# Hybrid decoder step on one Trainium2 core: elementwise work moved from GpSimd to VectorE and ScalarE

## The chip, the cores and the metric

The kernel runs on one core of one Trainium2 chip. The core has five engines that run side by side and wait for each other through semaphores: TensorE (PE in the profile; its weight loads are PEld), VectorE (DVE), ScalarE (ACT), GpSimd (POOL) and SyncE (SP), whose queue issues the kernel's DMAs. The metric is the time of one execution on the device in microseconds (us), smaller is better.

## What is computed

One layer of a decoder over a prompt of 2048 tokens (width 1024) and one decode step for 8 samples. Cut to what matters here:

```
h = rmsnorm(x, g_norm1) * (1 + sc1) + sh1
qkv, z, beta_in, a_in, aq, ak, av, iq, ik, iw = split(h @ w_in)
conv = silu(sum(w_conv[i] * xcat[:, i:i + t] for i in range(4)))   # xcat: three carried rows, then qkv
gq, gk, gv = split(conv); gq = l2norm(gq) * 128 ** -0.5; gk = l2norm(gk)
o_gdn, s_new = delta_rule(gq, gk, gv, g, beta, s0)                 # chunked, with a triangular solve
o_gdn = rmsnorm(o_gdn, g_gdn_norm) * silu(z)
aq, ak, iq, ik = partial_rope(...)
o_att = sparse_attn(aq, ak, av, iq, ik, iw)                        # scores, the best 256 keys, softmax
x = x + ga1 * (concat(o_gdn, o_att) @ w_out)
h2 = rmsnorm(x, g_norm2) * (1 + sc2) + sh2
gate, up = split(h2 @ w_ffn_in)
x = x + ga2 * ((silu(gate) * up) @ w_ffn_out)
```

Everything is float32. The large matrix products are made of two parts of each operand: a high part (the value as TensorE's float32r takes it) and a low part (the value minus its high part). Three products, high by high, high by low and low by high, are added up.

## The kernel before

**Tiling and staging.** The prompt is worked in four groups of 512 tokens. Phase 1 makes the modulation vectors, and for each group `project` (normalise, transpose, the input projection, the short convolution, rope) and `chunks` (the delta rule, in four chunks of 128 tokens, two of them interleaved). For the middle groups two blocks of attention (`first_attn`) and the later modulation vectors (`modulate`) stand between them. Phase 2 runs, for each group, the attention of the next four blocks of 128 tokens and then `ffn` (output projection, norm, SwiGLU, residual); the decode samples' attention and state step (`sample_steps`) stands ahead of the last `ffn`.

**Order.** All tiles come from pools with a fixed number of buffers per tag. The program is written in the order above, but a planner (`TileContext(schedule_with_timeline_sim=True)`) lays out each engine's instructions in an order that it finds by simulating the engines; then every engine works through its own list. An operation that changes its engine can therefore change the order of its neighbours.

**The weight path.** `weights` (L130 to L146) fetches a tile of 128 x 512 weights: SP loads it into `wr` (two buffers), ScalarE makes the high part with a cast (L141), GpSimd subtracts it for the low part (L142), both into `wi` (three buffers). The 56 tiles of the input projection are written back to DRAM in split form (`kept`) and only loaded for the later groups. The matmuls are those of `mm3` (L157 to L159), and of `mm_s` (L173, L174) for the few rows of the samples and the modulation. The buffer `wr` is free for the next load when the low part has been made.

**The steps around the change.** `norm_T` (L344) scales each row (L353), and for each of eight tiles transposes (L357), applies the modulation on VectorE into `ca` (two buffers, L359), casts on ScalarE (L360) and subtracts for the low part (L361). `conv` (L615) keeps three columns per channel block in `hist`; it puts them in front of the new columns in `raw` (L619, L620), saves the last three (L621), and does the four taps on VectorE (L624, L626). `rope` (L601) is four small operations on the rotated columns (L610 to L613). `tok` takes a block of projected tokens: for z it multiplies by the norm's gain (L645), and for the indexer queries it makes high and low parts of 256 columns (L689, L690) that TensorE then transposes (L694). `narrow` (L514) makes the gates in a chain of very small VectorE operations up to L553, which TensorE waits for at L559, and ropes the indexer keys.

`chunk` and `state` are the delta rule. A chunk transposes q, k and v (L729), squares them (L745), takes sums and a power (L747, L190), scales (L752, L754, L757), makes decay masks (L774, L776), builds a triangular matrix (L787, L788, L792, L793) and inverts it in six levels of matmuls (L800, L805, L806); `state` then updates the state (L849, L850) and normalises the output (L855 to L860).

**What stays.** The power of `rpow` (L190) stays on GpSimd, as do the low parts of the attention output (L1362) and of the gated hidden tile (L1425), and the residual adds of the FFN (L1353), each behind a VectorE multiplication (L1352).

Of the kernel before, what the change touches and what calls it, by code (L numbers as in the profile page):

```python
# [24 lines left out]
F32 = mybir.dt.float32  # L25
# [4 lines left out]
OP = mybir.AluOpType  # L30
# [10 lines left out]
H = 4  # L41
# [66 lines left out]
class K:  # L108
# [21 lines left out]
    def weights(self, src, key=None):  # L130

        nc = self.nc
        w = self.wp.tile([128, 2, 512], F32R, name="wi", tag="wi", bufs=WI)
        if key in self.kept:
            nc.sync.dma_start(w.bitcast(F32), self.kept[key])
            return w[:, 0], w[:, 1]
        wr = self.wp.tile([128, 512], F32, name="wr", tag="wr", bufs=WR)
        n = 512 // len(src)
        for j, s in enumerate(src):
            nc.sync.dma_start(wr[:, j * n:(j + 1) * n], s)  # L140
        nc.scalar.copy(w[:, 0], wr)  # L141
        nc.gpsimd.tensor_tensor(w[:, 1], wr, w[:, 0].bitcast(F32), op=OP.subtract)  # L142
        if key is not None:
            self.kept[key] = self.dr.tile([128, 2, 512], F32, name="kept")
            nc.sync.dma_start(self.kept[key], w.bitcast(F32))
        return w[:, 0], w[:, 1]  # L146
# [197 lines left out]
    def norm_T(self, pool, xt, nblk, Amul, Badd, hh, hl, tag, ptag, pbufs):  # L344

        nc = self.nc
        ss = pool.tile([128, nblk], F32, name=tag + "ss", tag=tag + "ss")
        for t in range(nblk):
            self.squares(pool, ss[:, t:t + 1], xt[:, t, :])
        r = self.rpow(pool, ss, nblk, 1.0 / D, EPS, tag)  # L350
        xn = xt
        for t in range(nblk):
            nc.vector.tensor_scalar(xn[:, t, :], xt[:, t, :], r[:, t:t + 1], None, op0=OP.mult)  # L353
        for k in range(KB):
            pt = self.ps.tile([128, 512], F32, name=ptag, tag=ptag, bufs=pbufs)
            for t in range(nblk):
                nc.tensor.transpose(pt[:, t * 128:(t + 1) * 128], xn[:, t, k * 128:(k + 1) * 128], self.id)  # L357
            h = self.p.tile([128, 512], F32, name="ca", tag="ca", bufs=2)
            nc.vector.tensor_scalar(h, pt, Amul[:, k, 0:1], Badd[:, k, 0:1], op0=OP.mult, op1=OP.add)  # L359
            nc.scalar.copy(hh[:, k, :], h)  # L360
            nc.gpsimd.tensor_tensor(hl[:, k, :], h, hh[:, k, :].bitcast(F32), op=OP.subtract)  # L361

    def norm_T_s(self, pool, xs, Amul, Badd, tag, ptag, pbufs):
        nc = self.nc
# [236 lines left out]
    def rope(self, x, tab, blk, rows, nh, half, tag):  # L601

        nc, p = self.nc, self.p1
        t = p.tile([128, 2, 8, 2, 8] if half == 8 else [128, 2, 4, 2, 16], F32, name="rope", tag="rope", bufs=1)
        xv = x[:, :, 0:2 * half].rearrange("p h (a c) -> p h a c", a=2)
        cosv = tab[:rows, blk, 0, :]
        b4 = lambda a: a.unsqueeze(1).unsqueeze(1).to_broadcast([rows, nh, 2, half])
        b3 = lambda a: a.unsqueeze(1).to_broadcast([rows, nh, half])
        pc, pn = t[:rows, 0, :nh], t[:rows, 1, :nh]
        nc.gpsimd.tensor_tensor(pc, xv, b4(cosv), op=OP.mult)  # L610
        nc.gpsimd.tensor_tensor(pn[:, :, 0, :], xv[:, :, 1, :], b3(tab[:rows, blk, 1, :]), op=OP.mult)
        nc.gpsimd.tensor_tensor(pn[:, :, 1, :], xv[:, :, 0, :], b3(tab[:rows, blk, 2, :]), op=OP.mult)
        nc.gpsimd.tensor_tensor(xv, pc, pn, op=OP.add)  # L613

    def conv(self, g, m, pd):  # L615

        nc, p = self.nc, self.p1
        raw = self.m("raw")
        nc.gpsimd.tensor_copy(raw[:, 0:3], self.hist[:, m, :])  # L619
        nc.scalar.copy(raw[:, 3:515], pd)  # L620
        nc.gpsimd.tensor_copy(self.hist[:, m, :], raw[:, 512:515])  # L621
        w = lambda i: self.cv[:, 64 + i * 12 + m:65 + i * 12 + m]
        a = self.p.tile([128, 512], F32, name="ca", tag="ca", bufs=2)
        nc.vector.tensor_scalar(a, raw[:, 0:512], w(0), None, op0=OP.mult)  # L624
        for i in range(1, 4):
            nc.vector.scalar_tensor_tensor(a, raw[:, i:i + 512], w(i), a, op0=OP.mult, op1=OP.add)  # L626
        th = self.th("cth")
        nc.scalar.activation(th, a, AF.Tanh, scale=0.5)
        nc.vector.scalar_tensor_tensor(th, th, 1.0, a, op0=OP.add, op1=OP.mult)
        nc.sync.dma_start(self.cT_d[g * 4:g * 4 + 4, :, m, :].rearrange("c p n -> p c n"), th.rearrange("p (c n) -> p c n", c=4))  # L630

    def tok(self, what, blk, pd, rows):
        nc, p, O = self.nc, self.p1, self.O
# [3 lines left out]
        if what == "z":  # L637
            th = self.th("cth")
            nc.scalar.activation(th[R], pd[R], AF.Tanh, scale=0.5)
            nc.vector.scalar_tensor_tensor(th[R], th[R], 1.0, pd[R], op0=OP.add, op1=OP.mult)  # L640
            if samp:
                nc.sync.dma_start(self.gzs_d, th[R])
            else:
                v = th.rearrange("p (h e) -> p h e", h=H)
                nc.gpsimd.tensor_tensor(v, v, self.gg.unsqueeze(1).to_broadcast([128, H, 128]), op=OP.mult)  # L645
                nc.sync.dma_start(self.gz_d[blk], th)
            return
        a = self.m("tk")[:, :512]
# [29 lines left out]
        else:  # L678
# [7 lines left out]
            for b in range(2):  # L686
                x = self.m("iqs", F32R)[:, :512].rearrange("p (h a c) -> p h a c", h=4, a=2)
                v = a[:, b * 256:(b + 1) * 256].rearrange("p (h c) -> p h c", h=4)
                nc.scalar.copy(x[:, :, 0, :], v)  # L689
                nc.gpsimd.tensor_tensor(x[:, :, 1, :], v, x[:, :, 0, :].bitcast(F32), op=OP.subtract)  # L690
                if b:
                    pt = self.ps.tile([128, 512], F32, name="d", tag="d", bufs=4)
                for h in range(4):
                    nc.tensor.transpose(pt[:, h * 128:(h + 1) * 128], x[:, h].bitcast(F32).rearrange("p a c -> p (a c)"), self.id)  # L694
                q = self.m("qo")[:, :512]
                nc.scalar.copy(q, pt)
                nc.sync.dma_start(self.iqT_d[blk, :, b * 512:(b + 1) * 512], q)
# [10 lines left out]
    def chunk(self, g, c, keep):  # L708

        nc, p = self.nc, self.p1  # L710
        n = g * 4 + c
        c4 = slice(c * 4, c * 4 + 4)
# [9 lines left out]
        v4 = lambda a: a.rearrange("p (h e) -> p h e", h=H)  # L722
        col = lambda a: a.unsqueeze(2).to_broadcast([128, a.shape[1], 128])
# [11 lines left out]
        qk = t("qk", 1024)  # L735
        v = t("v")
# [5 lines left out]
        yield  # L742
        kq = p.tile([128, H, 2, 128], F32, name="kq", bufs=2)
        sq = kq.rearrange("p h a e -> p (h a e)")
        nc.gpsimd.tensor_tensor(sq, qk, qk, op=OP.mult)  # L745
        ss = p.tile([128, 8], F32, name="ss8", bufs=2)
        nc.vector.tensor_reduce(ss, sq.rearrange("p (h e) -> p h e", h=8), op=OP.add, axis=AX.X)  # L747

        rn = self.rpow(p, ss, 8, 1.0, 4 * EPS, "rn")
        nc.vector.tensor_scalar(rn[:, 0:4], rn[:, 0:4], 128.0 ** -0.5, None, op0=OP.mult)  # L750
        qk8 = qk.rearrange("p (h e) -> p h e", h=8)
        nc.gpsimd.tensor_tensor(qk8, qk8, col(rn), op=OP.mult)  # L752
        qe = t("qe")
        nc.gpsimd.tensor_tensor(v4(qe), qk8[:, 0:4], col(self.gc[:, 3, c4]), op=OP.mult)  # L754
        yield
        kd = t("kd")
        nc.gpsimd.tensor_tensor(v4(kd), qk8[:, 4:8], col(self.gc[:, 4, c4]), op=OP.mult)  # L757
        transposed(lambda h: qk8[:, 4 + h, :], kq[:, :, 0, :], "s")
        yield
        transposed(lambda h: qk8[:, h, :], kq[:, :, 1, :], "v")  # L760
# [10 lines left out]
            nc.vector.tensor_scalar(dec[:, hs(h)], pg[:, hs(h)], self.gc[:, 2, c * 4 + h:c * 4 + h + 1], 0.0,  # L771
                                    op0=OP.add, op1=OP.min)
        nc.scalar.activation(dec, dec, AF.Exp)
        nc.gpsimd.tensor_tensor(v4(dec), v4(dec), self.u.unsqueeze(1).to_broadcast([128, H, 128]), op=OP.mult)  # L774
        decb = t("decb")
        nc.gpsimd.tensor_tensor(v4(decb), v4(dec), col(self.nbeta[:, c4]), op=OP.mult)  # L776
        yield
        NT, AT = t("NT"), t("AT")
        for a in range(2):
# [9 lines left out]
            yield  # L789

        E, Dm = t("E"), t("Dm")
        nc.gpsimd.tensor_tensor(v4(E), v4(NT), self.l1.unsqueeze(1).to_broadcast([128, H, 128]), op=OP.mult)  # L792
        nc.gpsimd.tensor_tensor(v4(E), v4(E), self.id.unsqueeze(1).to_broadcast([128, H, 128]), op=OP.add)  # L793
        transposed(lambda h: E[:, hs(h)], v4(Dm), "s")
        yield
        Y = t("Y")
# [15 lines left out]
    def state(self, g, c, kq, v, E, AT, qeT, kd):  # L812
# [33 lines left out]
        pu = P()  # L846
        for h in range(H):
            nc.tensor.matmul(pu[:, hs(h)], kd[:, hs(h)], vn[:, hs(h)], start=True, stop=True)
        nc.gpsimd.tensor_tensor(S2, S, col(self.gc[:, 5, c4]), op=OP.mult)  # L849
        nc.vector.tensor_tensor(S2, S2, v4(pu), op=OP.add)  # L850

        o = t("qe")
        nc.scalar.copy(o, po)
        sq2 = R
        nc.gpsimd.tensor_tensor(sq2, o, o, op=OP.mult)  # L855
        s4 = p.tile([128, 4], F32, name="ss4", bufs=2)
        nc.vector.tensor_reduce(s4, v4(sq2), op=OP.add, axis=AX.X)
        r4 = self.rpow(p, s4, 4, 1.0 / 128, EPS, "r4")
        nc.gpsimd.tensor_tensor(v4(o), v4(o), col(r4), op=OP.mult)
        nc.gpsimd.tensor_tensor(o, o, gz, op=OP.mult)  # L860
        oT = t("dec")
        pt = P()
        for h in range(H):
# [630 lines left out]
```

## Time and profile before

| | us |
|---|---|
| median of three runs | 4083.31 (4079.41 to 4086.87) |
| the profiled execution, whole | 4080.21 |
| its span, from the first to the last instruction | 4078.1 |

The profile is of one execution. Busy times are per engine; a share is of the span. In a group's row stand the source line, the engine, the operation, output <- inputs with their shapes, the count, the busy time in us and the mean in ns, and after the second bar the idle time of the engine just before these instructions, with what ended it. A wait's row reads: who waited <- for whom: us in total, times, longest. A stretch's row gives its two ends, its length, and the busy time of each engine in it with the number of instructions, then the granted TensorE clock (1.00 is full speed), the share of the DMA engines and their GB/s.

### The profile page before, as it was taken

The numbers are of one execution on the slowest core, as the hardware profiler recorded it, in microseconds if no ns is written. First come the engines' busy times: TensorE is split into PE (matmuls) and PEld (weight loads), VectorE is DVE, ScalarE is ACT, GpSimd is POOL, SyncE is SP. The second block draws the span as 40 slices with busy tenths as digits, with TensorE's granted clock in tenths as the row PEclk, the third lists the DMA queues.
The fourth block names the chain that finished last, engine by engine and source line by source line (L and its number), as shares of the span: only waits on it lengthen the run. The fifth ranks groups of instructions, "written<-read, shape, count | busy, mean of one in ns | idle before, by whom it ended". The sixth has DMA issues, their size and how long they took to land. (4 is left out here: it accounts for less than half of the span.)

```text
span 4078.1 us, 51174 instructions
## 1 busy us (share of the span) xinstructions
PE 3699.3 (91%) x17420; PEld 2852.2 (70%) x17420; DVE 1873.0 (46%) x3492; ACT 1357.3 (33%) x2583; POOL 1992.0 (49%) x1897
## 2 busy tenths in 40 slices
PE   8888988899798879999998999998999996889997
PEld 4766877777686657677776777876877754467775
DVE  2423432441355223866668757387671238022123
ACT  2233223322332333333344443344433331132222
POOL 3366234432621575544564555564555552246555
PEclk9899999999899889999999999999999996989998
DMA  6653453373346334355535333234333333332222
GB/s 233 209 204 118 128 199 113 118 239 132 124 157 215 103 94 139 101 145 163 154 105 172 92 95 102 88 119 162 93 103 101 91 101 126 133 100 81 80 78 71
DMA packets 368313, 528.21 MB, mean 130 GB/s; under 512 B 45612, under 2 KB 246353, under 8 KB 365986
## 3 DMA queue, kind: packets, MB, share of 16 engines
q1 hardware_dynamic: 368042, 524.86, 40.5%
q8 instruction: 139, 2.28, 0.2%
q14 instruction: 132, 1.08, 0.1%
HBM read 427.33 MB, written 116.36 MB: 133 GB/s over the span
## 5 line engine op out<-in xcount | busy, mean ns | idle before, releaser
L142 POOL TENSOR_TENSOR wi<-wr,wi 128x512 fp32r<-128x512 f32 x712 | 937.6, 1323 | 1060.3 <-ACT wi L141 1030.7
L141 ACT CAST wi<-wr 128x512 fp32r<-128x512 f32 x712 | 439.5, 620 | 1118.7 <-PE d L159 345.6
L157 PE MATMUL d<-hh,wi 128*128 128x512 f32 x1792 | 736.0, 411 | 23.4 <-DVE tm L1352 7.0
L158 PE MATMUL d<-hl,wi 128*128 128x512 f32 x1792 | 717.2, 400 | 0.0
L159 PE MATMUL d<-hh,wi 128*128 128x512 f32 x1792 | 653.4, 403 | 0.0
L157 PEld LDWEIGHTS d<-hh,wi 128*128 128x128 f32 x1792 | 339.6, 190 | 118.9 <-DVE tm L1352 11.3
L159 PEld LDWEIGHTS d<-hh,wi 128*128 128x128 f32 x1792 | 338.3, 189 | 89.1 <-issue 6.7
L158 PEld LDWEIGHTS d<-hl,wi 128*128 128x128 f32 x1792 | 339.5, 189 | 77.5 <-issue 5.5
L1353 POOL TENSOR_TENSOR xt<-xt,tm 128x512 f32<-128x512 f32 x224 | 302.4, 1366 | 50.5 <-DVE tm L1352 34.3
L157 PE MATMUL d<-wi,hh 128*128 128x512 f32 x768 | 297.2, 411 | 24.5 <-DMA wi<-kept 15.5
L1245 DVE SCALAR_TENSOR_TENSOR sc<-rl,iw,sc 128x512 f32<-128x512 f32 (+3 forms) x224 | 222.2, 992 | 196.3 <-ACT rl L1238 187.4
L158 PE MATMUL d<-wi,hh 128*128 128x512 f32 x768 | 308.9, 402 | 0.2 <-POOL wi L142 0.2
L159 PE MATMUL d<-wi,hl 128*128 128x512 f32 x768 | 306.0, 400 | 0.0
L158 PE MATMUL d<-wi,ah 128*128 128x512 f32 x704 | 275.9, 395 | 0.9 <-POOL wi L142 0.9
L159 PE MATMUL d<-wi,al 128*128 128x512 f32 x704 | 271.4, 397 | 0.0
L157 PE MATMUL d<-wi,ah 128*128 128x512 f32 x704 | 256.5, 407 | 7.6 <-ACT ah L1424 3.6
L1352 DVE TENSOR_TENSOR tm<-d,row 128x512 f32<-128x512 f32 x224 | 150.1, 685 | 221.9 <-PE d L159 160.4
L1419 DVE SCALAR_TENSOR_TENSOR th<-th,d 128x512 f32<-128x512 f32 x88 | 58.1, 682 | 373.5 <-ACT th L1418 373.3
L806 DVE COPY_PREDICATED Dm<-cl,g 128x512 f32<-128x512 uint8 x96 | 70.0, 731 | 312.0 <-PE g L805 311.8
L1238 ACT ACTIVATE rl<-s 128x512 f32<-128x512 f32 (+3 forms) x288 | 148.1, 543 | 149.2 <-PE s L1236 110.4
L1139 DVE TENSOR_SCALAR_CACHE_REDUCE bias<-sc,sv 128x640 bf16<-128x640 f32 (+11 forms) x120 | 193.3, 1611 | 3.2
L157 PEld LDWEIGHTS d<-wi,hh 128*128 128x128 f32 x768 | 146.5, 192 | 66.4 <-DMA wi<-kept 17.8
(504 smaller groups left out, 6398.7 us busy)
## 6 DMA issues: line engine op xcount, KB each, us to landing
wr<-in_w_ffn_in_dram SPq DMA_DIRECT2D x704, 128.0 KB, 2.3
wi<-kept SPq DMA_DIRECT2D x168, 512.0 KB, 4.1
wr<-in_w_ffn_out_dram SPq DMA_DIRECT2D x176, 256.0 KB, 2.7
kept<-wi SPq DMA_DIRECT2D x56, 512.0 KB, 2.9
xt<-in_x_prompt_dram SPq DMA_DIRECT2D x8, 2048.0 KB, 7.6
wr<-in_w_ada_dram SPq DMA_DIRECT2D x64, 256.0 KB, 2.8
wr<-in_w_out_dram SPq DMA_DIRECT2D x64, 256.0 KB, 2.6
wr<-in_w_in_dram SPq DMA_DIRECT2D x56, 256.0 KB, 3.7
```

The source lines that it names most:

```text
L141: nc.scalar.copy(w[:, 0], wr)
L142: nc.gpsimd.tensor_tensor(w[:, 1], wr, w[:, 0].bitcast(F32), op=OP.subtract)
L157: nc.tensor.matmul(out, wh, xh, start=start, stop=False, **kw)
L158: nc.tensor.matmul(out, wh, xl, start=False, stop=False, **kw)
L159: nc.tensor.matmul(out, wl, xh, start=False, stop=stop, **kw)
L806: nc.vector.copy_predicated(v4(Dm), self.cl[:, lv, :].unsqueeze(1).to_broadcast([128, H, 128]), v4(pp))
L1139: nc.vector.tensor_scalar(c, s, t, None, op0=OP.is_ge, op1=OP.add, accum_out=cnt)
L1238: nc.scalar.activation(r[:, :w], ps[:, :w], AF.Relu)
L1245: nc.vector.scalar_tensor_tensor(s, r[:, :w], iw, s, op0=OP.mult, op1=OP.add)
L1352: nc.vector.tensor_tensor(tm[:rows], pd[:rows], rw, op=OP.mult)
L1353: nc.gpsimd.tensor_tensor(xt, xt, tm[:rows], op=OP.add)
L1419: nc.vector.scalar_tensor_tensor(th, th, 1.0, pd[j], op0=OP.add, op1=OP.mult)
```

## The change

Twenty lines of GpSimd work go to VectorE: the low part of the weights (L142) and of the normalised tile (L361), the four operations of rope (L610 to L613), the gain of z (L645), the low part of the indexer queries (L690), and in the delta rule L745, L752, L754, L757, L774, L776, L792, L793, L849, L855, L859 and L860. The two copies of the convolution's carry (L619, L621) go to ScalarE, and the second one reads the matmul's result in PSUM rather than the copied tile. Operands and shapes of the moved operations stay the same.

```diff
-        nc.gpsimd.tensor_tensor(w[:, 1], wr, w[:, 0].bitcast(F32), op=OP.subtract)
+        nc.vector.tensor_tensor(w[:, 1], wr, w[:, 0].bitcast(F32), op=OP.subtract)
...
-            nc.gpsimd.tensor_tensor(hl[:, k, :], h, hh[:, k, :].bitcast(F32), op=OP.subtract)
+            nc.vector.tensor_tensor(hl[:, k, :], h, hh[:, k, :].bitcast(F32), op=OP.subtract)
...
-        nc.gpsimd.tensor_tensor(pc, xv, b4(cosv), op=OP.mult)
+        nc.vector.tensor_tensor(pc, xv, b4(cosv), op=OP.mult)
...
-        nc.gpsimd.tensor_copy(raw[:, 0:3], self.hist[:, m, :])
+        nc.scalar.copy(raw[:, 0:3], self.hist[:, m, :])
         nc.scalar.copy(raw[:, 3:515], pd)
-        nc.gpsimd.tensor_copy(self.hist[:, m, :], raw[:, 512:515])
+        nc.scalar.copy(self.hist[:, m, :], pd[:, 509:512])
...
-                nc.gpsimd.tensor_tensor(v, v, self.gg.unsqueeze(1).to_broadcast([128, H, 128]), op=OP.mult)
+                nc.vector.tensor_tensor(v, v, self.gg.unsqueeze(1).to_broadcast([128, H, 128]), op=OP.mult)
...
-                nc.gpsimd.tensor_tensor(x[:, :, 1, :], v, x[:, :, 0, :].bitcast(F32), op=OP.subtract)
+                nc.vector.tensor_tensor(x[:, :, 1, :], v, x[:, :, 0, :].bitcast(F32), op=OP.subtract)
...
-        nc.gpsimd.tensor_tensor(sq, qk, qk, op=OP.mult)
+        nc.vector.tensor_tensor(sq, qk, qk, op=OP.mult)
...
-        nc.gpsimd.tensor_tensor(v4(E), v4(NT), self.l1.unsqueeze(1).to_broadcast([128, H, 128]), op=OP.mult)
-        nc.gpsimd.tensor_tensor(v4(E), v4(E), self.id.unsqueeze(1).to_broadcast([128, H, 128]), op=OP.add)
+        nc.vector.tensor_tensor(v4(E), v4(NT), self.l1.unsqueeze(1).to_broadcast([128, H, 128]), op=OP.mult)
+        nc.vector.tensor_tensor(v4(E), v4(E), self.id.unsqueeze(1).to_broadcast([128, H, 128]), op=OP.add)
...
-        nc.gpsimd.tensor_tensor(S2, S, col(self.gc[:, 5, c4]), op=OP.mult)
+        nc.vector.tensor_tensor(S2, S, col(self.gc[:, 5, c4]), op=OP.mult)
```

The lines of rope and of the delta rule that aren't printed here change in the same way.

More of the change, by code (lines that the diff above doesn't have):

```diff
@@ L609, in rope @@
         pc, pn = t[:rows, 0, :nh], t[:rows, 1, :nh]
-        nc.gpsimd.tensor_tensor(pc, xv, b4(cosv), op=OP.mult)
-        nc.gpsimd.tensor_tensor(pn[:, :, 0, :], xv[:, :, 1, :], b3(tab[:rows, blk, 1, :]), op=OP.mult)
-        nc.gpsimd.tensor_tensor(pn[:, :, 1, :], xv[:, :, 0, :], b3(tab[:rows, blk, 2, :]), op=OP.mult)
-        nc.gpsimd.tensor_tensor(xv, pc, pn, op=OP.add)
+        nc.vector.tensor_tensor(pc, xv, b4(cosv), op=OP.mult)
+        nc.vector.tensor_tensor(pn[:, :, 0, :], xv[:, :, 1, :], b3(tab[:rows, blk, 1, :]), op=OP.mult)
+        nc.vector.tensor_tensor(pn[:, :, 1, :], xv[:, :, 0, :], b3(tab[:rows, blk, 2, :]), op=OP.mult)
+        nc.vector.tensor_tensor(xv, pc, pn, op=OP.add)
     def conv(self, g, m, pd):
@@ L751, in chunk @@
         qk8 = qk.rearrange("p (h e) -> p h e", h=8)
-        nc.gpsimd.tensor_tensor(qk8, qk8, col(rn), op=OP.mult)
+        nc.vector.tensor_tensor(qk8, qk8, col(rn), op=OP.mult)
         qe = t("qe")
-        nc.gpsimd.tensor_tensor(v4(qe), qk8[:, 0:4], col(self.gc[:, 3, c4]), op=OP.mult)
+        nc.vector.tensor_tensor(v4(qe), qk8[:, 0:4], col(self.gc[:, 3, c4]), op=OP.mult)
         yield
         kd = t("kd")
-        nc.gpsimd.tensor_tensor(v4(kd), qk8[:, 4:8], col(self.gc[:, 4, c4]), op=OP.mult)
+        nc.vector.tensor_tensor(v4(kd), qk8[:, 4:8], col(self.gc[:, 4, c4]), op=OP.mult)
         transposed(lambda h: qk8[:, 4 + h, :], kq[:, :, 0, :], "s")
@@ L773, in chunk @@
         nc.scalar.activation(dec, dec, AF.Exp)
-        nc.gpsimd.tensor_tensor(v4(dec), v4(dec), self.u.unsqueeze(1).to_broadcast([128, H, 128]), op=OP.mult)
+        nc.vector.tensor_tensor(v4(dec), v4(dec), self.u.unsqueeze(1).to_broadcast([128, H, 128]), op=OP.mult)
         decb = t("decb")
-        nc.gpsimd.tensor_tensor(v4(decb), v4(dec), col(self.nbeta[:, c4]), op=OP.mult)
+        nc.vector.tensor_tensor(v4(decb), v4(dec), col(self.nbeta[:, c4]), op=OP.mult)
         yield
@@ L854, in state @@
         sq2 = R
-        nc.gpsimd.tensor_tensor(sq2, o, o, op=OP.mult)
+        nc.vector.tensor_tensor(sq2, o, o, op=OP.mult)
         s4 = p.tile([128, 4], F32, name="ss4", bufs=2)
@@ L858, in state @@
         r4 = self.rpow(p, s4, 4, 1.0 / 128, EPS, "r4")
-        nc.gpsimd.tensor_tensor(v4(o), v4(o), col(r4), op=OP.mult)
-        nc.gpsimd.tensor_tensor(o, o, gz, op=OP.mult)
+        nc.vector.tensor_tensor(v4(o), v4(o), col(r4), op=OP.mult)
+        nc.vector.tensor_tensor(o, o, gz, op=OP.mult)
         oT = t("dec")
```

## The prediction

> **What bounds the kernel now.** I read the page's busy lines first, then the busy table over chosen stretches, then PE's waits, then the groups by form for prices.
>
> ```profile
> span 4078.1 us, 51174 instructions
> PE 3699.3 (91%) x17420; PEld 2852.2 (70%) x17420; DVE 1873.0 (46%) x3492; ACT 1357.3 (33%) x2583; POOL 1992.0 (49%) x1897
> ```
>
> PE is busy for 91% of the span, so at most 4078.1 - 3699.3 = 379 us could be won by feeding it better. VectorE (DVE) and GpSimd (POOL) are each busy about half of the time, but not in the same stretches (columns: the stretch and its length, then PE, PEld, DVE, ACT and POOL busy, granted clock, DMA share, GB/s):
>
> ```profile
> 0.00:1600.00 1600.00, 1390.53 (x7454) 1118.25 (x7455) 574.91 (x1255) 489.96 (x987) 697.70 (x863) 0.93 0.47 157
> 350.00:400.00 50.00, 31.72 (x205) 26.67 (x205) 24.82 (x45) 18.21 (x36) 43.35 (x47) 0.83 0.18 56
> 700.00:750.00 50.00, 39.02 (x201) 29.19 (x201) 18.37 (x37) 18.67 (x32) 44.63 (x38) 0.83 0.47 144
> 1050.00:1100.00 50.00, 36.72 (x195) 27.87 (x196) 17.00 (x36) 18.85 (x32) 44.29 (x38) 0.86 0.51 156
> 1440.00:1490.00 50.00, 34.24 (x154) 23.40 (x154) 12.91 (x34) 16.98 (x30) 45.17 (x38) 0.77 0.36 106
> 1600.00:3300.00 1700.00, 1631.81 (x7099) 1260.72 (x7098) 1049.26 (x1844) 663.16 (x1207) 907.10 (x706) 0.99 0.39 118
> 2100.00:2300.00 200.00, 181.91 (x797) 136.70 (x796) 165.30 (x299) 94.51 (x183) 106.90 (x78) 0.98 0.42 138
> 2800.00:2900.00 100.00, 93.14 (x400) 69.71 (x399) 85.23 (x149) 45.89 (x85) 39.37 (x31) 0.95 0.40 129
> 2900.00:3000.00 100.00, 100.00 (x430) 78.30 (x430) 69.92 (x107) 38.85 (x67) 56.79 (x43) 1.00 0.31 92
> ```
>
> Of the 379 us, 209 lie in the first 1600 us (projections, delta rule, modulation) and 68 in the next 1700 (attention beside the FFN). Four **seams** of 50 us in the first stage, between one group's projection and the next, have POOL 87 to 90% busy and PE at 63 to 78%, with the granted clock down to 0.77: there POOL is the bound. From 1600 on PE is the bound, and DVE comes nearest to a second one: 83% in 2100-2300 and 85% in 2800-2900.
>
> **The change part by part.** First the prices: each row has its count, then busy us and mean ns.
>
> ```profile
> L142 POOL TENSOR_TENSOR wi<-wr,wi 128x512 fp32r<-128x512 f32 x712 | 937.6, 1323 | 1060.3 <-ACT wi L141 1030.7 <-DMA wr<-in_w_ffn_in_dram 7.8 <-DMA kept<-wi 5.8
> L752 POOL TENSOR_TENSOR qk<-qk,rnz 128x1024 f32<-128x1024 f32 x16 | 30.3, 1896 | 0.3
> ```
>
> ```profile
> L850 DVE TENSOR_TENSOR S<-S,s 128x512 f32<-128x512 f32 x16 | 11.0, 685 | 43.5 <-PE s L848 43.5
> L747 DVE TENSOR_REDUCE ss<-kq 128x8 f32<-128x1024 f32 x16 | 19.4, 1215 | 4.9 <-POOL kq L745 4.9
> L787 DVE TENSOR_TENSOR NT<-g,decb 128x256 f32<-128x256 f32 x32 | 13.5, 422 | 43.2 <-POOL decb L776 23.4 <-PE g L782 19.9
> L592 DVE TENSOR_TENSOR iks<-ik,iks 128x128 fp32r<-128x128 f32 x16 | 5.3, 330 | 1.1 <-ACT iks L591 1.1
> L549 DVE TENSOR_TENSOR spw<-spw 128x16 f32<-128x16 f32 x21 | 3.6, 171 | 0.5
> ```
>
> A moved 128x512 operation goes from 1.32 us on POOL (L142) to about 0.685 on DVE (L850; it reads one input from PSUM, and L592 and L549 with both inputs in SBUF lie on the same slope), a 128x1024 one from 1.90 to about 1.215, 256 columns to 0.42. DVE gains 712 (L142) + 64 (L361) + 160 (ten lines of the delta rule x16) + 16 (L645) = 952 x 0.685 = 652 us, 32 x 1.215 = 39 (L745, L752), 32 x 0.42 = 13 (L690), and for the 64 ropes of four small operations, between 0.17 and 0.33 each, about 62: 766 us in all. That makes 1873 + 766 = 2639, 65% of the span; over the whole run DVE isn't full. What counts is each stage.
>
> *Seams and waits for POOL.* PE's longest waits in the first 1600 us (total us, times, longest):
>
> ```profile
> PE d L694 <- POOL iqs L690: 27.0, 6, 6.8
> PE d L174 <- POOL wi L142: 19.6, 15, 2.9
> ...
> PE g L729 <- POOL qk L752: 16.4, 9, 5.1
> PE d L559 <- DVE gt L553: 13.9, 1, 13.9
> PE d L173 <- ACT wi L141: 10.9, 15, 1.8
> ...
> PE g L729 <- POOL E L793: 9.1, 5, 4.8
> ```
>
> The POOL waits and the L173 wait behind them are 83.0 us. If these are serial chains, they shrink as their operations do, to about 0.55 (0.685/1.323 and 1.215/1.896, mixed): 46% of 83 = 38 us gone, and the low clock that goes with the gaps gives a little more; 46 as an outer end. If they are load, the seams' work only changes engines: DVE gets 0.55 x POOL on top of its own, 24.8 + 23.8 = 48.6 of 50 where POOL had 43.4, then 42.9 for 44.6, 41.4 for 44.3 and 37.8 for 45.2; in sum 170.7 for 177.4, a gain of 7 us, and the first seam even loses 5. A wait in front of a single L694 is a chain, but DVE's queue now carries the two chunks, the ropes and the weights in one order, and each wait for ScalarE that POOL used to sit out holds them all. I take a point between the ends, **-25** (ends -46 and +5).
>
> *The narrow chain.* L559's 13.9 us are DVE working through a chain of tiny operations. The key ropes add 5 x 4 operations of 0.171 us to the same queue: **+3** (0 to +3.4). For groups 1 to 3 other matmuls hide it.
>
> *norm_T.* DVE makes the scaled tile (0.81 us) and now the low part too: 1.49 us per tile. Today POOL sets that pace, as two of its low parts start 3598.94 and 3601.79, 2.85 us apart:
>
> ```profile
> 3598.94 2.49 POOL L361 TENSOR_TENSOR hl<-ca,hh 128x512 fp32r<-128x512 f32 x2 [0.35 <-ACT hh L360]
> ...
> 3601.47 0.81 DVE L359 TENSOR_SCALAR ca<-d,A,mod 128x512 f32<-128x512 f32 x1 [0.41 <-POOL hl L361]
> 3601.79 2.49 POOL L361 TENSOR_TENSOR hl<-ca,hh 128x512 fp32r<-128x512 f32 x2 [0.35 <-ACT hh L360]
> ```
>
> So 1.43 becomes 1.49 (0.81 + 0.685), 64 times: **+4** (0 to +4).
>
> *The carry.* 96 copies of three columns go to ScalarE.
>
> ```profile
> L621 POOL COPY hist<-raw 128x3 f32<-128x3 f32 x48 | 17.2, 365 | 165.3 <-ACT raw L620 164.5
> ```
>
> ```profile
> L1435 ACT COPY acs<-g 128x16 f32<-128x16 f32 x11 | 1.9, 172 | 58.9 <-PE g L1434 58.9
> ```
>
> At 0.172 us each they are 16.5 us of an engine that is 31% busy in this stage: nothing, hidden beside matmuls (8 us, 48 x 0.172, if each stood ahead of a convolution PE waits for). L621 kept POOL waiting 165 us with other work behind it; that is part of the seam term.
>
> *The weight path from 1600 on.* The low parts of L142 in three stretches (POOL busy and count), and one DVE line in two stages:
>
> ```profile
> 1600.00:3300.00 1700.00, 556.69 (x417) 0.99 0.39 118
> 2100.00:2300.00 200.00, 55.96 (x38) 0.98 0.42 138
> 2800.00:2900.00 100.00, 20.93 (x16) 0.95 0.40 129
> ```
>
> ```profile
> L1245 DVE SCALAR_TENSOR_TENSOR sc<-rl,iw,sc 128x512 f32<-128x512 f32 x167 | 176.2, 1055 | 155.3 <-ACT rl L1238 149.2 <-ACT ah L1424 0.5
> ...
> L1245 DVE SCALAR_TENSOR_TENSOR ct<-decb,iw,ct 128x512 f32<-128x512 f32 x7 | 5.2, 742 | 0.1
> ```
>
> With 32 of norm_T's, 449 low parts x 0.685 = 308 us of DVE arrive here. The same L1245 takes 1.055 us in this stage and 0.742 in the first, where POOL works little beside it: two-input DVE operations wait for POOL ones. With most of POOL's work gone up to 167 x 0.313 = 52 us come back. DVE goes from 1049 to about 1305 of 1700, 77%. A low part that lands 0.64 us sooner also frees its raw buffer sooner, and the load of the next one is issued from SP's queue only then, with the loads of keys, values and attention outputs behind it. Against that stands the order: behind a low part that waits for ScalarE's cast now stand the score, softmax and eviction operations that PE needs. Gain: no more than the 68 us that PE idles here, and I set its end at 25, half of the returned 52; loss: 68 (the third rival). The nearest row is 2900-3000, where DVE is at 70% and PE has no idle time; I take **+5** (-25 to +68).
>
> By the Trainium skill, page SBUF — State Buffer, section "Who interferes with whom", a VectorE operation with two SBUF inputs blocks against a GpSimd one that reads SBUF, for its whole duration. By that rule a moved low part would itself be held by what stays on POOL, above all the residual adds of L1353: POOL keeps up to 907.1 - 556.7 = 350 us of the 1700 (21%), and half of a 1.3 us operation for 21% of 417 low parts is, as an estimate, 57 us, as much as the 52 that come back; the term would be about +15 and the sum -6. The 1.055 against 0.742 agrees with the rule; no row shows a moved operation.
>
> *The tail.* In the last stretch the residual adds share POOL with L142 no longer: **-3** (two or three operations of 1.32 us between adds; 0 to -4).
>
> Sum: -25 + 3 + 4 + 5 - 3 = **-16**. The profiled execution took 4080.2 us (span 4078.1 and 2.1 around it), 3.1 below the median 4083.3 of three. 4080.2 - 16 = 4064, on the median **4067**.
>
> **The rivals.**
> 1. *The seams open wide.* The chain end holds (-46), and PE's 141.7 us in the four seams, granted 0.82 on average, run at full clock (141.7 x 0.18 = 25 less), with a relief of 10 from 1600 on: 4083 - 81 = about 4002. For it: POOL near 90% there. Against it: DVE's 48.6 of 50.
> 2. *Nothing measurable.* PE's waits are renamed from POOL to DVE, and PE's matmuls set the time: 4083, give or take 8. For it: 177.4 against 170.7.
> 3. *Slower: one queue for too much.* DVE's operations follow one another in the planner's order, and from 1600 on the low parts stand among evictions and selection. If one low part per group of matmuls comes later than PE wants it, by one operation of 0.685 us, that is about 100 groups (224 evictions L1352 in fours, 88 gates L1419 in twos) = 68 us: 4151. It decides where DVE's share passes about 95%: 2100-2300 gets 38 tiles, 165.3 + 26 = 191 of 200; 2800-2900 gets 16, 85.2 + 11 = 96 of 100, before the relief.
>
> The Trainium skill speaks for this rival: Perfetto Trace Analysis, section "Optimizing Scalar/DVE Operations", says that where DVE is saturated, moving work to ScalarE or even GpSimd may pay, the reverse of this change; it would give the 4151. The trace shows DVE near saturation in 300 us only.
>
> That the change does less than it says can't be: every moved line changes engine; only the planner's new order is open.
>
> **How the numbers follow.** A measurement of this kernel can tell about 0.2% (8 us) from no change. Chances: forecast 0.38 (its own range 4045 to 4075), rival 1 0.16, rival 2 0.16, rival 3 0.30. Faster 0.54, same 0.16, slower 0.30. The range 3990 to 4130 takes in rival 1 but for its far end, rival 2, and the nearer half of rival 3.
>
> **What would show it.** Right: L142 on DVE at about 0.69 us; L1245 near 0.75; PE's waits for POOL under 15 us; POOL below 650 us, DVE between 2500 and 2640; PE's idle time under 190 us before the FFN starts. Wrong: PE waiting for DVE wi by tens of us, DVE over 95% for 200 us and more, clock dips in stretches that had 1.00 before.

## The result and the profile after

The changed kernel takes 4015.55 us (median of four runs, 4008.01 to 4019.66), the kernel before 4081.36 in the same comparison: a ratio of 0.9836, with a 95% interval of 0.9816 to 0.9857. That is 66 us or 1.6% faster. The profiled execution took 4017.87 us, and its page begins:

```profile
span 4016.0 us, 50754 instructions
PE 3688.3 (92%) x17420; PEld 2837.9 (71%) x17420; DVE 2439.4 (61%) x4780; ACT 1365.8 (34%) x2679; POOL 618.4 (15%) x513
```

TensorE's work is the same 17420 matmuls, POOL has lost 1374 us and DVE has only gained 566. To see where the 62 us of the span come from, I cut both profiles at the same pieces of work instead of at the same microseconds. The marks are the end of the first gate chain (L553: 113 us before, 111 after), the first gated tile of the FFN (L1424, 1615 and 1534) and the first gated tile of the last group (3634 and 3573). The busy table of the kernel before between these marks, then that of the changed kernel (columns as in the prediction):

```profile
113.00:1615.00 1502.00, 1321.20 (x7154) 1081.39 (x7155) 541.24 (x1173) 463.88 (x927) 669.63 (x810) 0.94 0.46 152
1615.00:3634.00 2019.00, 1884.97 (x8147) 1415.36 (x8146) 1182.52 (x2074) 737.95 (x1355) 1017.30 (x810) 0.96 0.39 120
```

```profile
111.00:1534.00 1423.00, 1292.55 (x7124) 1060.38 (x7125) 799.09 (x1826) 468.64 (x1012) 81.70 (x57) 0.96 0.49 160
1534.00:3573.00 2039.00, 1902.37 (x8173) 1420.90 (x8172) 1399.24 (x2548) 739.90 (x1356) 413.61 (x342) 0.95 0.38 119
```

The first row of each is phase 1: 1502 us became 1423, a gain of 79, and 2 more lie ahead of it. Length minus PE busy is PE's idle time: 180.8 became 130.5, so 50 of the 79 are idle time. The other 29 are PE being busy for less time with almost the same matmuls: 30 of them (some 5 us at 0.185 each) were placed later, into phase 2, and the remaining 23 or so go with the granted clock, 0.94 before and 0.96 after. The second row is phase 2 up to the last FFN: 2019 became 2039, so 20 us are lost there, although POOL is relieved by 600 us; where they are lost is shown with the experiments. Behind the last mark both take the same (444 and 443).

What PE waited for in phase 1 of the changed kernel (who waited <- for whom: us in total, times, longest):

```profile
PE d L157 <- DMA wi<-kept: 15.2, 13, 5.4
PE d L173 <- ACT wi L141: 13.8, 18, 1.4
PE d L559 <- DVE gt L553: 12.6, 1, 12.6
PE g L729 <- DVE Dm L806: 11.8, 19, 1.9
...
PE d L694 <- DVE iqs L690: 5.8, 7, 1.1
```

No wait for POOL is left in this stretch. Summed over all rows of this view, the waits for POOL and DVE together went from 131 us (84 for POOL, 48 for DVE) to 86, all for DVE. So they were not just renamed.

The groups of the changed kernel answer to the prices in the prediction:

```profile
L142 DVE TENSOR_TENSOR wi<-wr,wi 128x512 fp32r<-128x512 f32 x712 | 530.4, 749 | 696.1 <-ACT wi L141 686.1 <-DMA wr<-in_w_ada_dram 2.9 <-DMA kept<-wi 2.1
L1245 DVE SCALAR_TENSOR_TENSOR sc<-rl,iw,sc 128x512 f32<-128x512 f32 x167 | 145.1, 869 | 54.3 <-ACT rl L1238 48.7 <-DVE sc L1245 0.9 <-ACT wi L141 0.5
L752 DVE TENSOR_TENSOR qk<-qk,rnz 128x1024 f32<-128x1024 f32 x16 | 19.5, 1220 | 0.2
L690 DVE TENSOR_TENSOR iqs<-tk,iqs 128x256 fp32r<-128x256 f32 x32 | 14.4, 450 | 6.9 <-ACT iqs L689 6.9
L849 DVE TENSOR_TENSOR S<-S,gc 128x512 f32<-128x512 f32 x16 | 10.9, 681 | 0.0
```

The moved operations cost about what was forecast, but for L142 (0.749 in the mean in place of 0.685; its median is 0.691). And the four seams, at the same distances from the marks as in the prediction's table:

```profile
329.00:379.00 50.00, 36.40 (x265) 31.77 (x264) 42.61 (x89) 21.43 (x44) 7.69 (x5) 0.93 0.19 63
669.00:719.00 50.00, 40.56 (x221) 30.31 (x218) 44.53 (x85) 21.33 (x37) 6.40 (x3) 0.86 0.52 169
1002.00:1052.00 50.00, 40.28 (x237) 29.38 (x238) 45.14 (x88) 21.33 (x37) 8.25 (x4) 0.93 0.53 165
1359.00:1409.00 50.00, 40.37 (x244) 29.76 (x242) 39.17 (x73) 21.59 (x39) 6.87 (x4) 0.91 0.41 121
```

DVE is busy 171.4 of these 200 us (170.7 were forecast), about as full as POOL was, and still PE works 157.6 us where it worked 141.7, at a clock of 0.91 in place of 0.82. An engine that is 86% busy in a stretch need not be the bound of the stretch.

### The profile page after: what moved, and what is told of

Its sections match the earlier page's. It is cut to its first block, busy times and chain, and to the rows that moved or that the text cites. A ratio compares the mean times of both kernels' runs of the same rounds, so it can differ in the third digit from the quotient of the medians.

```text
span 4016.0 us, 50754 instructions
## 1 busy us (share of the span) xinstructions
PE 3688.3 (92%) x17420; PEld 2837.9 (71%) x17420; DVE 2439.4 (61%) x4780; ACT 1365.8 (34%) x2679; POOL 618.4 (15%) x513
## 4 chain that ended last, share of the span: by engine, by line
PE 66%; DVE 16%; DMA 8%; issue 4%; ACT 3%; SPq 2%; POOL 1%; ACTq 0%; DVEq 0%; POOLq 0%
PE d L157 16%; PE d L158 15%; PE d L159 15%; PE g L1304 2%; PE s L1236 2%; DVE wi L142 2%; PE g L800 2%; PE s L1279 1%; PE g L805 1%; DMA wi<-kept 1%; PE g L729 1%; DVE bias L1139 1%; DMA wr<-in_w_ada_dram 1%; PE g L1298 1%; DMA wr<-in_w_ffn_in_dram 1%
## 5 line engine op out<-in xcount | busy, mean ns | idle before, releaser
L142 DVE TENSOR_TENSOR wi<-wr,wi 128x512 fp32r<-128x512 f32 x712 | 530.4, 749 | 696.1 <-ACT wi L141 686.1
L1353 POOL TENSOR_TENSOR xt<-xt,tm 128x512 f32<-128x512 f32 x224 | 325.2, 1470 | 527.5 <-DVE tm L1352 424.3
L1425 POOL TENSOR_TENSOR al<-ca,ah 128x512 fp32r<-128x512 f32 x88 | 120.6, 1388 | 1086.4 <-ACT ah L1424 1074.8
L158 PE MATMUL d<-wi,ah 128*128 128x512 f32 x704 | 281.4, 401 | 0.6 <-DVE wi L142 0.5
L157 PE MATMUL d<-wi,ah 128*128 128x512 f32 x704 | 267.6, 415 | 12.1 <-DVE th L1419 4.6
L1245 DVE SCALAR_TENSOR_TENSOR sc<-rl,iw,sc 128x512 f32<-128x512 f32 (+3 forms) x224 | 182.1, 813 | 62.6 <-ACT rl L1238 55.2
L1236 PE MATMUL s<-ik,iqT 128*128 128x512 f32 (+3 forms) x576 | 162.6, 387 | 18.5 <-ACT rl L1238 16.1
```

Source lines behind the costliest of these rows:

```text
L142: nc.vector.tensor_tensor(w[:, 1], wr, w[:, 0].bitcast(F32), op=OP.subtract)
L157: nc.tensor.matmul(out, wh, xh, start=start, stop=False, **kw)
L158: nc.tensor.matmul(out, wh, xl, start=False, stop=False, **kw)
L1236: nc.tensor.matmul(ps[:, :w], iq[:, h, :].bitcast(F32R), B["ikT"][c * 2 + a][:, :w].bitcast(F32R), start=a == 0, stop=a == 1)
L1245: nc.vector.scalar_tensor_tensor(s, r[:, :w], iw, s, op0=OP.mult, op1=OP.add)
L1353: nc.gpsimd.tensor_tensor(xt, xt, tm[:rows], op=OP.add)
```

## The experiments

The whole is a median, the ratio that to the kernel before on the same chip, with its 95% interval; "phase 1" is the time from the end of the first gate chain to the first gated tile, "phase 2" from there to the first gated tile of the last group.

| kernel | whole | ratio to before | phase 1 | phase 2 | POOL busy in phase 1 |
|---|---|---|---|---|---|
| before | 4081.4 | 1 | 1502 | 2019 | 670 |
| carry_only | 4094.1 | 1.0023 (1.0008 to 1.0038) | 1502 | 2033 | 647 |
| iqs_only | 4083.7 | 1.0007 (0.9995 to 1.0020) | 1489 | 2036 | 649 |
| z_only | 4101.1 | 1.0049 (1.0035 to 1.0063) | 1515 | 2025 | 650 |
| proj_only | 4035.2 | 0.9879 (0.9860 to 0.9898) | 1443 | 2042 | 484 |
| wi_only | 4033.3 | 0.9880 (0.9862 to 0.9898) | 1453 | 2024 | 508 |
| delta_only | 4028.6 | 0.9863 (0.9845 to 0.9880) | 1452 | 2017 | 459 |
| delta_load | 4043.0 | 0.9904 (0.9884 to 0.9924) | 1466 | 2005 | 559 |
| wi_back | 4039.2 | 0.9890 (0.9872 to 0.9909) | 1449 | 2037 | 259 |
| pool_load | 4032.5 | 0.9879 (0.9864 to 0.9894) | 1431 | 2030 | 165 |
| dve_load | 4028.5 | 0.9861 (0.9841 to 0.9881) | 1430 | 2035 | 79 |
| p1_all | 4019.8 | 0.9835 (0.9812 to 0.9858) | 1422 | 2036 | 125 |
| wi_p1 | 4009.6 | 0.9814 (0.9797 to 0.9830) | 1421 | 2032 | 112 |
| after | 4015.6 | 0.9836 (0.9816 to 0.9857) | 1423 | 2039 | 82 |

**One part at a time.** Three kernels make one part of the change each:

```diff
wi_only: L142 alone
-        nc.gpsimd.tensor_tensor(w[:, 1], wr, ...)
+        nc.vector.tensor_tensor(w[:, 1], wr, ...)
delta_only: the twelve lines of L745 to L860, each as
-        nc.gpsimd.tensor_tensor(qk8, qk8, col(rn), op=OP.mult)
+        nc.vector.tensor_tensor(qk8, qk8, col(rn), op=OP.mult)
proj_only: L361, L610 to L613, L645, L690 to VectorE, L619 and L621 to ScalarE
```

> Only the low part of the weights (L142) goes to VectorE, all else as before. By the marks of the two profiles the change gains 81 us up to the first gated tile of the feed-forward stage (L1424, 1615 to 1534), 22 more up to the end of the third group (3322 to 3219), and loses 42 in the stretch of the sample steps that follows. Theory A (phase 1 is a matter of POOL's own chains and load in the delta rule and the projections; phase 1 has 263 low parts of 1.32 us, about 347 of POOL's 698 us there): L142 alone takes half of POOL's load off, so about half of the 81: the first gated tile at about 1575, the whole about 4040. Theory B (two-input VectorE operations are held by POOL's low parts, and these run all the time): nearly all of it, first gated tile at 1545 or earlier, the whole 4000 to 4025. Theory C (no place is special, the planner's new order makes the gain): any time, with no link to the waits that name POOL.

> Only the twelve lines of the delta rule (L745 to L860) go to VectorE, L142 and the projections' lines stay on GpSimd, the carry too. Theory A: 160 operations of 1.32 us and 32 of 1.90 leave POOL (272 us), and PE's 25 us of waits for qk and E with them; the first gated tile at about 1575, the whole about 4040, so that wi_only and delta_only share the gain about evenly. Theory B: little, the first gated tile later than 1600, the whole 4065 to 4085, since the low parts stay on POOL and the moved operations are held by them (L752 well over its 1.22 us).

> Only the lines of the projections (L361, rope, L645, L690) go to VectorE and the carry (L619, L621) to ScalarE. The largest wait of PE for POOL, 27 us in front of L694, ends with L690. Theory A: -20 to -30 (27 us of L694, less 4 for norm_T and 3 for the narrow chain): 4050 to 4060. Theory B: within 8 us of before.

(The count of 263 low parts in phase 1 is wrong: it took in those of the first FFN and of the end. The weight tiles of phase 1 number 120, as the 240 idle operations of pool_load, two per tile, show.) Each part alone gained 49 to 59 us of phase 1 and 1.2 to 1.4% of the whole. None of the theories had that: A's times for wi_only and delta_only were near (first gated tile at 1575 for 1564 and 1567), but it expected parts that add up to the whole, and they add up to 158 of 79; B expected nearly all of it from wi_only and nothing from proj_only, which gained most of the three in phase 1. What remains of B is a price: with the low parts still on POOL, the moved operations of delta_only are longer than the 1220 ns above.

```profile
L752 DVE TENSOR_TENSOR qk<-qk,rnz 128x1024 f32<-128x1024 f32 x16 | 22.7, 1417 | 0.4
```

**Is it only the planner's order?** Three small moves change the instruction lists but hardly POOL's load. In z_only nothing moves that PE waits for; iqs_only ends the largest wait of the kernel before (L694, 27.0 us); carry_only takes away what kept POOL's queue waiting for ScalarE.

```diff
carry_only: L619 and L621
-        nc.gpsimd.tensor_copy(raw[:, 0:3], self.hist[:, m, :])
+        nc.scalar.copy(raw[:, 0:3], self.hist[:, m, :])
iqs_only: L690
-                nc.gpsimd.tensor_tensor(x[:, :, 1, :], v, ...)
+                nc.vector.tensor_tensor(x[:, :, 1, :], v, ...)
z_only: L645
-                nc.gpsimd.tensor_tensor(v, v, self.gg..., op=OP.mult)
+                nc.vector.tensor_tensor(v, v, self.gg..., op=OP.mult)
```

> Only the carry's copies (L619, L621) go to ScalarE, with nothing else changed: 96 copies that keep POOL busy for some 25 us. The three runs of one part each gained 51, 48 and 59 us up to the first gated tile, and the whole change 81, so the parts don't add. Theory T1 (POOL's load was the bound of phase 1's seams, and any part that brings it below the bound gains most of the rest): almost nothing here, 0 to -10, for POOL is relieved of 25 us alone. Theory T2 (head of POOL's queue: L621 waited 165 us for ScalarE with other work behind it): -20 to -45 by the first gated tile. Theory T3 (the planner's order): not foreseeable, up to 50 either way.

> Only the low part of the indexer queries (L690, 32 operations of 256 columns) goes to VectorE: about 25 us of POOL's load, and the largest wait of PE for POOL (27.0 us in 6 waits). T1: 0 to -10. T2 (single chains and what heads the queue): -15 to -27, for L694 no longer stands behind POOL's queue. T3: not foreseeable.

> A control: only the gain of z (L645, 16 operations of 1.3 us) goes to VectorE. PE does not wait for it, and it is 21 us of 698 on POOL. The planner's lists change all the same. T1 and T2: within 8 us of before, the first gated tile at 1605 to 1625. T3: as far from before as the other single parts, 20 to 50 us.

Phase 1 came to 1502, 1489 and 1515 (1502 before): in these three the order moved it by up to 13 us either way, not by 50. T3 is not borne out as the cause of the gain. z_only lies outside T1's 8 us, with 13 us more in phase 1 and some 20 in the whole, and iqs_only is 2 us past T1's 10; both may be the order. T2 is not borne out either: with the carry's copies off POOL phase 1 is not a microsecond shorter, and the 13 us of iqs_only are less than T2's 15 and no more than the order gave z_only. In iqs_only PE's wait at L694 was mostly renamed, from 27.0 us for POOL to

```profile
PE d L694 <- DVE iqs L690: 20.6, 9, 3.5
```

In z_only L694 waits for POOL only 10.2 us, but the squares and scales of the delta rule wait instead:

```profile
PE g L729 <- POOL qk L752: 41.8, 11, 7.7
```

(16.4 before). Which line stands in the table of waits is the order's choice, and their sum moves with the order too: PE's waits for POOL and DVE in phase 1 come to 160 us in z_only and 131 before. T1 stands so far.

**Load that nobody reads.** If POOL's load is the cause, adding load without lengthening any chain must cost time. In pool_load and delta_load GpSimd subtracts constants twice for each weight tile of phase 1, in dve_load VectorE does it four times, each into a tile `idle` of its own; pool_load and dve_load stand on the changed kernel, delta_load on delta_only. Two lines of pool_load:

```diff
+        for i in range(0 if hasattr(self, "p2") else 2):
+            nc.gpsimd.tensor_tensor(self.idle, self.cf[:, 0:160], self.cf[:, 512:672], op=OP.subtract)
```

> The whole change, and in phase 1 two more GpSimd subtractions of 128x160 for each weight tile, on constants, whose result nobody reads (some 500 operations, an estimated 250 us on POOL in phase 1). Nobody queues behind them but the power (L190) and the first stages' few POOL operations. If VectorE is slowed by what runs on POOL beside it (theory B, the ports), its two-input operations grow and the first gated tile comes at 1560 or later, the whole 4040 or more. If what counts is who waits for POOL (T1, T2), 4012 to 4025.

> The kernel with only the delta rule moved (4028.6 us, first gated tile at 1567), and in phase 1 two GpSimd subtractions of 128x160 on constants for each weight tile, read by nobody: 240 operations, 164 us where the whole change carried them. No chain is longer by them, only POOL's queue is fuller again. T1 (POOL's load in phase 1 was the bound, with what queues behind it): most of the 48 us that delta_only gained up to the first gated tile is lost again, first gated tile at 1595 to 1620, the whole 4060 to 4090. Its rival T4 (what counted is that the moved operations are shorter, so that their chains are): within 12 us of delta_only, 4028 to 4040.

> The whole change, and in phase 1 four VectorE subtractions of 128x160 on constants for each weight tile, read by nobody (480 operations of an estimated 0.25 us, 120 us). VectorE is 86% busy in the four seams of the changed kernel. If that is near its bound as POOL's 89% was before: first gated tile 20 us later or more, the whole 4036 and up. If VectorE still has room: within 10 us of the changed kernel, 4015 to 4026.

The idle operations did not run where they were meant to. Nobody waits for their results, and the planner put them all ahead of the four seams, but for the last few of dve_load; three of the four groups got none. The rows of pool_load, delta_load and dve_load (shortest, median and longest in ns, then the first and the last start in us):

```profile
L144 POOL TENSOR_TENSOR idle<-cf x240: 510/532/2212, 29.3 to 215.4; 128x160 f32<-128x160 f32 x120
L144 POOL TENSOR_TENSOR idle<-cf x240: 511/530/1591, 29.4 to 298.5; 128x160 f32<-128x160 f32 x120
L144 DVE TENSOR_TENSOR idle<-cf x480: 249/324/1022, 29.0 to 362.1; 128x160 f32<-128x160 f32 x160
```

In all three the first gates come at 123 to 125 us, 10 to 14 later than without, and 119, 87 and 141 of the idle operations run before them; so phase 1 is counted from there, and only the whole contains that delay. Busy tables of phase 1, of pool_load, delta_only, delta_load and dve_load:

```profile
123.00:1554.00 1431.00, 1298.38 (x7129) 1066.55 (x7130) 816.55 (x1829) 468.26 (x1014) 165.42 (x178) 0.96 0.48 159
```

```profile
115.00:1567.00 1452.00, 1305.69 (x7175) 1070.10 (x7176) 689.84 (x1373) 465.56 (x939) 458.85 (x622) 0.96 0.49 160
```

```profile
125.00:1591.00 1466.00, 1306.45 (x7174) 1075.16 (x7174) 700.88 (x1373) 467.89 (x939) 558.77 (x776) 0.95 0.48 158
```

```profile
124.00:1554.00 1430.00, 1292.53 (x7130) 1062.75 (x7131) 895.76 (x2169) 469.74 (x1014) 79.32 (x57) 0.96 0.48 159
```

84 us more on POOL came with 8 us more than in the changed kernel, and lengthened DVE's busy time by 17 without any new DVE work; 100 us more came with 14 over delta_only, 97 us more on DVE with 7. None of these three clearly exceeds the 13 us that the order alone made, so they give no price for a microsecond of load. The first group, where the load ran, says more. From the first gates to those of the second group it took 328 us in delta_only, 348 in delta_load and 345 in the kernel before (344 to 353 in the three small moves). These 20 us are all that delta_only had gained in that group, and PE's waits for POOL rose in it from 9 to 28 us, those for the low parts of the weights (L142) from 1 to 11. In pool_load, where PE waited for nothing on POOL, the same group took 333 us for 326, though POOL was 90% busy from 125 to 215 us. So in the first group load on POOL costs time where work that PE waits for queues behind it, as T1 has it, and little where none does.

The other three groups, with three of the seams, got no load: there delta_load took 1118 us for the 1124 of delta_only, against 1157 before. So its whole, 14 us over delta_only, lies between T4's 12 and T1's range and decides nothing about them, and dve_load doesn't show that DVE had room in the seams. The wholes of pool_load and dve_load fell between their two ranges each, with 12 to 14 us of late start in them. Nor is the gain even in POOL's load: from 670 to some 480 us on POOL phase 1 falls by 49 to 59, from 484 to 259 (proj_only, wi_back) not at all, from 259 to 82 by 26. How much is POOL's load and how much the shorter moved operations is not settled.

**The whole change without L142, and phase 1 alone.** Three kernels start from the changed one:

```diff
wi_back: L142 on GpSimd throughout
-        nc.vector.tensor_tensor(w[:, 1], wr, ...)
+        nc.gpsimd.tensor_tensor(w[:, 1], wr, ...)
wi_p1: L142 on GpSimd from phase 2 on; p1_all: L361 as well
-        nc.vector.tensor_tensor(w[:, 1], wr, ...)
+        (nc.gpsimd if hasattr(self, "p2") else nc.vector).tensor_tensor(w[:, 1], wr, ...)
```

> The whole change but the low part of the weights (L142), which stays on GpSimd throughout. T1: POOL keeps some 160 us of low parts in phase 1, far from its bound, so the first gated tile comes at 1535 to 1550, though L142 alone had gained 51 us from the kernel before; the whole 4010 to 4035 (phase 2 as scattered as in the runs so far, 2017 to 2042 us from the first gated tile of group 0 to that of group 3). If the parts added, L142 would be worth its 51 here too: first gated tile at 1585, the whole 4065.

> The whole change, but L142 is on VectorE only in phase 1 and on GpSimd from phase 2 on. Phase 1 should be as in after (first gated tile at 1534, give or take 8). If the 42 us lost in the stretch of the sample steps come from low parts that stand in VectorE's queue there, they come back, and the 22 us gained before are lost: about 3995, faster than after. If the loss lies with the planner's order whatever the engine of L142, it stays and the whole is 4035 or so.

> The whole change in phase 1 only: from phase 2 on the low parts of the weights and of norm_T (L142, L361) are on GpSimd as before. The first gated tile at 1532 to 1540. Phase 2 is then the one of the kernel before with another order. If the 20 us that the changed kernel lost between the first gated tiles of group 0 and group 3 (2039 for 2019) come from VectorE's low parts: 2019, the whole about 3996. If they are the scatter of the planner's order, which three kernels without any edit in phase 2 showed too (2025, 2033, 2036): 2017 to 2042, the whole 3995 to 4018.

The parts overlap: L142 is worth 49 us of phase 1 as the first part moved and 26 as the last (1449 to 1423), less than the 51 of parts that add and more than the 1 to 16 that T1 allowed. For phase 2, the busy table of p1_all:

```profile
1537.00:3573.00 2036.00, 1900.67 (x8150) 1420.59 (x8149) 1198.56 (x2076) 739.84 (x1356) 1017.18 (x811) 0.96 0.38 119
```

It has the work of the kernel before on every engine (POOL 1017 and 1017, DVE 1199 and 1183), and its phase 2 is 17 us longer than that one's and 3 shorter than that of the changed kernel, which has 604 us less on POOL and 201 more on DVE. carry_only, iqs_only and z_only, with no edit in phase 2, got 2033, 2036 and 2025. So over the whole of phase 2 the engine of the low parts is worth nothing that shows, and the 20 us lost there lie within the spread of all these kernels (2005 to 2042); the kernel before has one of the better orders.

The sum hides two opposite shifts. Cut at the last gated tile of the third group, phase 2 has three groups of attention and FFN and then the stretch of the sample steps. Before, and after:

```profile
1615.00:3322.00 1707.00, 1638.85 (x7117) 1260.51 (x7116) 1049.12 (x1843) 667.23 (x1215) 902.04 (x703) 0.99 0.39 118
3322.00:3634.00 312.00, 246.12 (x1032) 154.84 (x1031) 133.39 (x231) 70.72 (x142) 115.26 (x108) 0.82 0.38 127
```

```profile
1534.00:3219.00 1685.00, 1623.94 (x7084) 1258.94 (x7083) 1240.45 (x2283) 661.65 (x1202) 345.74 (x271) 0.99 0.39 119
3219.00:3573.00 354.00, 278.43 (x1091) 161.96 (x1091) 158.79 (x265) 78.26 (x155) 67.87 (x72) 0.78 0.34 115
```

The first stretch gained 22 us, the second lost 42, with 59 more matmuls in it. In wi_p1 both went back, to 1717 and 315: that is the first branch of its expectation, though the whole, 4009.6, came between the two figures named, 3995 and 4035. The four kernels with L142 on VectorE in phase 2 have 1671 to 1690 and 343 to 355, and all others 1686 to 1718 and 312 to 330, except proj_only, which has 1682 and 360 with L142 on GpSimd. So an order with more work in the sample steps goes mostly with L142 on VectorE, but doesn't need it, and which of the two costs the time stays open.

wi_p1 has the lowest median, 6 us under the changed kernel; the intervals overlap, and p1_all, which differs from it by 32 operations, is 4 us above the changed kernel. No version is shown to beat it.

## Why the prediction was right in its sign and small in its size

The forecast was 4067 (-16 us), 4015.6 came (-66), outside the forecast's own 4045 to 4075. It lies inside the range only because the range reached down to take in rival 1; the sum itself had a quarter of the gain. Step by step:

- *Prices.* Right: 0.683 (L361), 0.681 (L849), 1.220 (L752), 0.450 (L690; 0.42 forecast). L142 took 0.749, and 0.697 for the 120 tiles of p1_all's phase 1, with GpSimd nearly empty beside them.
- *Relief of DVE.* Far too small. It was counted for L1245 alone, 52 us; L1245 x167 gave 31 (176.2 to 145.1). But all 3492 instructions that did not move, added up one by one, gave 156: 2032 us before, 1877 after. The moved ones took 816 us for the 766 forecast, but one operation's end overlaps the next one's start (all of DVE's durations add up to 2692 us, its busy time is 2439), and busy time rose by only 566. For both reasons the range of 2500 to 2640 for DVE missed (2439).
- *Seams and waits, -25 (ends -46 and +5).* This is the term that failed in size: 81 us were gained up to the first gated tile. Idle time in phase 1 fell by 50, already past the end of -46 that shorter chains gave, and some 23 more came from PE's busy time with the granted clock. The forecast allowed for the clock with "a little more"; only rival 1 priced it, at 25. The reason for the middle value, that DVE would be as full as POOL (170.7 for 177.4), was right in its numbers (171.4) and wrong in what followed: a DVE at 86% left 16 us more of PE work in the same 200 us.
- *Where.* The four seams were taken for the place. PE's idle time in them fell from 58.3 to 42.4 us, 16 of the 50; the other 34 lie between them.
- *Narrow chain, norm_T, carry, tail.* +3, +4, 0, -3 forecast. L559's wait went from 13.9 to 12.6; carry_only showed 1502 for 1502 in phase 1; the tail took 443 for 444. norm_T wasn't measured by itself.
- *Weight path, +5 (-25 to +68).* The term was set for 1600 to 3300, and there 22 us were gained, near the end of -25. The 42 us lost in the sample steps behind it had no term. wi_p1 and p1_all, with L142 on GpSimd in phase 2, lost 13 and 17 us in phase 2 all the same. The forecast had no term for the planner's new order, which is worth more than this step.
- *The signs.* PE's waits for POOL are gone from phase 1 and come to 6 us in the whole run (below 15), POOL is at 618 (below 650), PE's idle time ahead of the first gated tile is 159 (below 190), PE waits 5.0 us for DVE's wi (L174). L1245 stayed at 0.869, not 0.75. From the first gated tile to the end of the third group the clock is 0.99 in both kernels, so the dips named as a sign of being wrong didn't come.
- *The rivals.* Rival 1 was nearest in size: it had -46 and -25 where phase 1 gave -50 of idle time and some -23 with the clock. That is in part luck: its 25 were for seams at full clock, and they run at 0.91, with 16 of the 50 us in them. Its 10 from phase 2 came as 20 the other way, 4002 against 4015.6. Rival 2 falls by the sum of the waits (131 to 86). Rival 3's mechanism doesn't show: DVE reached 92% in the fullest 200 us (2600 to 2800), and the same phase 2 came out with the low parts on POOL.

```profile
2600.00:2800.00 200.00, 183.14 (x795) 135.98 (x794) 183.14 (x325) 90.42 (x170) 42.49 (x33) 0.99 0.43 140
```

The rule of the Trainium skill, page SBUF — State Buffer, section "Who interferes with whom", was weighed with 57 us of delay for the low parts in phase 2. In the stretch from 1534 to 3219 they are these:

```profile
L142 DVE TENSOR_TENSOR wi<-wr,wi 128x512 fp32r<-128x512 f32 x417 | 311.7, 752 | 293.2 <-ACT wi L141 289.0 <-PE d L159 1.5 <-PE s L1236 0.6
```

By that rule the sum was -6; against L361's 0.683 they lost 417 x 0.069 = 29 us, half of the estimate. The trace agrees with the rule's direction, and it did not decide the time.

## What to carry to other kernels

Price the granted clock with the idle time: where waits break TensorE's stream, the time that comes back was about half as large again as the idle time itself (73 us for 50, without the 5 us of matmuls that were placed later). Try the parts of a change one by one and last as well as first: here each part alone gave 60 to 75% of the whole gain of phase 1, and small moves gave at most 13 us, which the order alone can give, so neither a list of waits nor a sum of parts would have told the worth. Look up in the trace where an added load ran before reading its price: here the planner put it ahead of the place that it was meant to test. Where a planner writes the order, measure a few edits that should do nothing before reading anything into 20 us.

## What was not expected of the hardware

GpSimd's work lengthened even the smallest VectorE operations. The scaling of four columns (L750) before, and after:

```profile
L750 DVE TENSOR_SCALAR rnz<-rnz 128x4 f32<-128x4 f32 x16 | 11.3, 708 | 25.9 <-POOL rnz L190 25.9
```

```profile
L750 DVE TENSOR_SCALAR rnz<-rnz 128x4 f32<-128x4 f32 x16 | 2.6, 163 | 4.6 <-POOL rnz L190 4.6
```

Nothing of the operation changed, and its mean fell from 708 to 163 ns; the one-column L1141, most of which runs in phase 2, went from 439 to 275. p1_all, with GpSimd relieved in phase 1 alone, has 167 for L750 and 479 for L1141, so each follows what GpSimd does in its own phase. Over the whole run 1374 us taken off POOL took 156 us off the VectorE instructions that did not move, 0.11 for each us; in pool_load DVE's busy time grew by 17 for 84 us, 0.20. So a VectorE share read beside a busy GpSimd holds time that is waiting, and it shrinks when the work is moved.
